# One group of the down projection's weight sums per up step

## The chip, the cores and the metric

One core of one Trainium2 chip runs the whole kernel as one program. The metric is device time in microseconds, the median of several runs. The engines are named as in the profile: PE (TensorE, matrix products; PEld is its loading of weights), DVE (VectorE), ACT (ScalarE), POOL (GpSimd) and SP (SyncE, which here only issues transfers). Each engine works off its own queue in order and waits on semaphores of the others.

## The reference

One inference step of a decoder layer, float32, for 1024 new prompt tokens and 8 decode tokens (1032 columns). Cut to what matters here:

```python
h = rmsnorm(x, norm1_w); proj = h @ w_in               # 1024 -> 6672
...                                                    # two recurrences: Mamba-2 (SSD) and HGRN2, 8 heads
x = x + concat([o_a, y]) @ w_out                       # 2048 -> 1024
h = rmsnorm(x, norm2_w)
gate, val = split(h @ w_up, 2)                         # 1024 -> 2 x 2816
gate = causal_dwconv(gate, ...)                        # width 3
x = x + (silu(gate) * val) @ w_down                    # 2816 -> 1024
y = rmsnorm(x, final_norm_w)
```

The kernel also returns the recurrent and convolution states.

## The kernel before, in words

Activations lie transposed, features on the 128 partitions and the 1032 tokens along the free axis. Each float32 product is made of three passes: a tile is split into a rounded part and a rest (`wh`/`wl` for weights, `uh`/`ul` for activations; ACT copies the rounded part, DVE subtracts it), and wh*uh, wh*ul and wl*uh are added up in PSUM.

The up and the down projection are made by a Strassen-like scheme: 2x2 blocks, seven products p1 to p7 in place of eight, on sums of blocks. The operands of four of the down projection's products (p6, p5, p4, p7) are sums of blocks of `w_down`. They are made ahead of time by `down_sums`: for each of 11 row-block pairs `i` and two halves `h` (22 groups) it loads four 128x256 blocks into the one buffer `wq` (tag "g", one buffer, which later holds the norm's `rst`), adds on POOL four times (L1202), and stores 512 KB to the scratch tensor `wsum_d` (L1204). The down projection reads `wsum_d` back (`dw_load`).

The order of the stages: the combined input projection with the SSD scan beside it; the eight HGRN2 heads, whose small products are put between the input projection's (`drive`); the output projection (jobs a, b, c, d0, d1); the up projection, 22 steps `j` of 128 gate and 128 value columns (`ups`); the down projection; the final norm.

One up step has 14 products of 12 matmuls, in the order p1, p6, p5, p7, p2, p4, p3, each for both halves `i` of the tokens; `n` counts them from 0 to 13. p1, p7 and p3 use the PSUM tag "mm" (three banks, named `ua` in the profile), the others the tag "mx" (four banks, `ub`). DVE or ACT empties each bank (L1463 to L1498). `p7` also makes two subtractions on POOL (L1476, L1477), whose result the p3 product is added to (L1498). During a step the next one is prepared: `up_load(j + 1)` after n = 2 (two loads of 512 KB into `ws`), four sums of these weights on POOL (`up_sums`, L1417), and the splits of them (`up_split`, L1440 on ACT and L1441 on DVE) after n = 5, 9 and 13 and n = 1 of the next step. `up_close` then runs the convolution (L368, L370), SiLU and the gate product, and `act_sets` stores the activations' blocks to `act_d` (L1521).

The order on PE is written out by hand: it is the order of the code. On the other engines and on SP a planner orders the instructions by their place in the code, their due times and its own costs, so an instruction can stand in its queue ahead of one written before it. `tc.issue_after(x.ins)` around an instruction says that it comes after `x` in the queue of `x`'s engine, without a wait of its own. `fetch` issues a load behind the last weight load in SP's queue (`last_w`).

`tick` is called once for each matmul of a step and releases work queued with `after(n, ...)`; `spread(pieces, n)` runs one piece of a generator, and the next n ticks later. A job's step counts as a tick too. Before, `spread(down_sums(), 26)` is begun by the job "conv", ahead of the third head's input projection.

Of the kernel before, what the change touches and what calls it, by code (L numbers as in the profile page):

```python
# [13 lines left out]
ALU = mybir.AluOpType  # L14
# [3 lines left out]
P = 128  # L18
DM = 1024
# [15 lines left out]
DK = FT // 2  # L35
# [16 lines left out]
def hybrid_layer(  # L52
# [9 lines left out]
    V, A, G, PE, SP = nc.vector, nc.scalar, nc.gpsimd, nc.tensor, nc.sync  # L62
# [9 lines left out]
    def nm(s):  # L72
        cnt[0] += 1
        return f"{s}_{cnt[0]}"
# [8 lines left out]
    def tl(tag, name, dt=F32):  # L83
        w, n = TAGS[tag]
        return (work if tag in ("hT", "big", "e", "g") else tmp).tile([P, w], dt, tag=tag, bufs=n, name=nm(name))
# [104 lines left out]
    def fetch(dst, src):  # L190

        with tc.issue_after(last_w[0].ins):
            SP.dma_start(dst, src)  # L193
# [44 lines left out]
    def job(name, load, run):  # L238
        jobs.append((name, load, run))

    def after(n, work):

        item = [n, work]
        later.append(item)
        return item
# [14 lines left out]
    def spread(pieces, n, then=None):  # L260

        def go():
            if next(pieces, 0) is None:
                after(n, go)
            elif then is not None:
                then()
        go()
# [75 lines left out]
    def conv_state(src2d, nrow, ntile, out):  # L343
        def rows(j0):
            rt = half("rt")
            nj = min(4, ntile - j0)
            fetch(rt[:nrow, :nj * P], src2d[:, j0 * P:(j0 + nj) * P])
            return rt, nj

        nxt = rows(0)  # L350
        for j0 in range(0, ntile, 4):
            yield
            (rt, nj), nxt = nxt, rows(j0 + 4) if j0 + 4 < ntile else None
            ps = bank("cst", "nx")
            for j in range(nj):
                PE.transpose(ps[:, j * nrow:(j + 1) * nrow], rt[:nrow, j * P:(j + 1) * P], ident[:nrow, :nrow])
            V.tensor_copy(out[:, j0:j0 + nj, :], ps[:, :nj * nrow].rearrange("p (j r) -> p j r", r=nrow))
# [120 lines left out]
    for i in range(9):  # L478
        n = P if i < 8 else ND
# [285 lines left out]
    def ssm_conv_state():  # L765
        for j0 in range(0, XT, 4):
            yield
            ps = bank("l11", "nx")
            for j in range(4):
                PE.transpose(ps[:11, j * P:(j + 1) * P], last11[:, j0 + j, :], ident)  # L770
            csr = keep.tile([16, 512], F32, tag="csr", bufs=1, name=nm("csr"))
            V.tensor_copy(csr[:11, :512], ps[:11, :])
            cl = slice(j0 * P, (j0 + 4) * P)
            SP.dma_start(cs_prompt[0, 0, :, cl], csr[0:3, :512])
            SP.dma_start(cs_sample[0, :, 2, cl], csr[3:11, :512])
        SP.dma_start(cs_sample[0, :, 0:2, :], state_conv_ssm[0, :, 1:3, :])
# [16 lines left out]
    def once(work):  # L793
        def run():
            work()
            return
            yield
        return run
# [63 lines left out]
    def head_in(h):  # L862
        t = {}

        def f_end():
            f, k = t["f"], tl("big", "k")
            A.activation(f[:, :NT], f[:, :NT], AF.Identity, bias=lbt[:, 0, h:h + 1], scale=lbt[:, 1, h:h + 1])
            V.tensor_scalar(k[:, :NT], f[:, :NT], -1.0, 1.0, op0=ALU.mult, op1=ALU.add)
            t["k"] = k

        for n, off, func in (("f", OFF_F, AF.Sigmoid), ("q", OFF_Q, AF.Silu), ("v", OFF_I, AF.Copy),
                             ("sg", OFF_G, AF.Silu)):
            def evict(c, cs, ps, n=n, func=func):
                t["out"] = A.activation(t[n][:, cs], ps, func)

            def begin(n=n):
                t[n] = tl("e" if h == 0 and n == "f" else "big", n)

            if h == H - 1 and n == "sg":
                in_job_last(f"{n}{h}", off + h * P, evict, begin)  # L880
            else:
                in_job(f"{n}{h}", off + h * P, evict, begin, f_end if n == "f" else None)
        return t
# [305 lines left out]

    wsum_d = dram.tile([2, 4, 2, P, DK, P], F32, name="wsum_d")  # L1190

    def down_sums():
        src = w_down[0].rearrange("(i two p) (gv h c) -> h i p two gv c", two=2, p=P, gv=2, h=2)
        for i in range(DK):
            for h in range(2):
                t = tl("g", "wq")[:, :DM]
                for two in range(2):
                    fetch(t[:, two * 512:(two + 1) * 512].rearrange("p (gv c) -> p gv c", gv=2), src[h, i][:, two])
                yield
                g1, v1, g2, v2 = (t[:, n * 256:(n + 1) * 256] for n in range(4))  # L1200
                for out, x_, y_ in ((v2, v1, v2), (v1, g1, v1), (g1, v2, g1), (g2, g1, g2)):
                    G.tensor_tensor(out, x_, y_, op=ALU.add)  # L1202
                yield
                SP.dma_start(wsum_d[h].rearrange("q m p k c -> p k (q m) c")[:, i],  # L1204
                             t.rearrange("p (q c) -> p q c", c=P))
                yield

    fbufT = keep.tile([P, FT, 16], F32, name="fbufT")

    def conv_states():  # L1210
        yield from ssm_conv_state()
        yield from conv_state(state_conv_ffn[0].rearrange("b r d -> (b r) d"), 16, FT, fbufT)
        yield
# [3 lines left out]
    heads[0] = head_in(0)  # L1217
    ssm_gate(1)
    heads[1] = head_in(1)
    job("conv", None, once(lambda: (spread(conv_states(), 60), spread(down_sums(), 26))))  # L1220
    for h in range(2, H):
        heads[h] = head_in(h)

# [170 lines left out]
    def up_load(j):  # L1394
        ws = []
        for c0 in (0, DFF):
            if j:
                t = wpool.tile([P, KT * P], F32, tag="ws", bufs=2, name=nm("ws"))
            else:
                t = tl("xv", "ws")[:, :KT * P]  # L1400
            last_w[0] = SP.dma_start(t.rearrange("p (k m) -> p k m", m=P),
                                     w_up[0, :, c0 + j * P:c0 + (j + 1) * P].rearrange("(k p) m -> p k m", p=P))
            ws.append(t)
        wraw[j] = ws
        if j > 1:
            up_sums(j)
# [20 lines left out]
    def up_split(j, n):  # L1427

        sums, ops_ = wparts[j]
        order = ORDER if j else FIRST  # L1430
        pool = tmp if n < 2 else wpool
        hi = pool.tile([P, KT * P], F32R, tag="wh", bufs=2, name=nm("wh"))
        lo = pool.tile([P, KT * P], F32R, tag="wl", bufs=2, name=nm("wl"))
        for i, name in enumerate(order[2 * n:2 * n + 2]):
            cs = slice(i * 512, (i + 1) * 512)
            if j == 1:
                with tc.issue_after(setmark[0].ins):
                    A.copy(hi[:, cs], sums[name])
            else:
                A.copy(hi[:, cs], sums[name])  # L1440
            V.tensor_tensor(lo[:, cs], sums[name], hi[:, cs].bitcast(F32), op=ALU.subtract)  # L1441
            ops_[name] = [t[:, cs].rearrange("p (k m) -> p k m", m=P) for t in (hi, lo)]

    class Up:
# [28 lines left out]
        def p7(self, ps):  # L1473
            self.u3 = tl("us", "us")
            V.tensor_tensor(self.u3, self.u2, ps, op=ALU.add)
            G.tensor_tensor(self.val[:, self.at(1)], self.f, self.u3, op=ALU.subtract)  # L1476
            G.tensor_tensor(self.u2, self.f, self.u2, op=ALU.subtract)  # L1477
            if hasattr(self, "late"):
                self.p4(self.late)

# [19 lines left out]
    def up_open(j):  # L1500
        ext, val = tl("xe", "fext"), tl("xv", "val")
        G.memset(ext[:, 0:2], 0.0)
        dreg = ext[:, 2 + T:2 + T + 24].rearrange("p (b r) -> p b r", r=3)
        G.tensor_copy(dreg[:, :, 0:2], fbufT[:, j, :].rearrange("p (b r) -> p b r", r=2))
        return [Up(j, i, ext, val) for i in range(2)]
# [143 lines left out]
    def ups(j, seq):  # L1649

        us_ = up_open(j)
        for n, (name, i) in enumerate(seq):
            yield from us_[i].mul(name)
            if n == 2 and j + 1 < FT:
                up_load(j + 1)
            if n == 5 and j == 0:
                up_sums(1)
            if n in (5, 9, 13) and j + 1 < FT:
                up_split(j + 1, (5, 9, 13).index(n))
            if n == 1 and j:  # L1660
                up_split(j, 3)
            if j == FT - 1:
                last_step(n)
        up_close(j, us_[0])

    with tc.manual_schedule(engines={mybir.EngineType.PE}):
# [26 lines left out]
        for _ in ups(0, [(name, i) for i in range(2) for name in FIRST]):  # L1693
            tick()
# [137 lines left out]
```

## Time and profile before

| | |
|---|---|
| time, median of 3 runs | 1749.66 us (1748.3 to 1752.6) |
| the profiled execution | 1748.51 us, span 1746.6 us |
| granted TensorE clock | 0.998 |
| PE busy | 1704.6 us (98%) |
| DVE busy | 1180.5 us (68%) |
| ACT busy | 838.3 us (48%) |
| POOL busy | 485.6 us (28%) |
| hardware DMA queue | 236.72 MB, 45.1% of 16 engines' span |

The span is the time from the first to the last instruction of the core; the rest of an execution lies around it. A row of a group of instructions names line, engine, operation, what it writes and reads, the shape and how many; then microseconds busy, the mean in nanoseconds, and the engine's idle time before them with what ended it. A row of the timeline begins with start and duration in microseconds. A row of waits names who waited for whom: total, times, longest. SPq rows are transfers being issued. The heads' stage runs from about 428 to 880 us of the span, the up steps from about 1054 to 1482, the down projection behind them.

### The profile page before, as it was taken

Reading aid. Unit: us, or ns where it says so; the run is one execution under the profiler, and the core shown is the slowest. Engines: PE = TensorE matmul, PEld = TensorE weight load, DVE = VectorE, ACT = ScalarE, POOL = GpSimd, SP = SyncE. Lnnn points to the kernel's source line nnn. Section 1 sums busy time; section 2 is a strip of 40 time slices with the busy share of each in tenths; the row PEclk is TensorE's granted clock in tenths of the full one; section 3 lists DMA queues with packets and bytes.
Section 4 is the critical chain, followed back from the end, with each engine's and each line's share of the span. In section 5 each row is a group of like instructions: output and inputs, shape, how many; then the busy total and the mean of one; then the engine's idle time right before and its main releaser. Section 6 shows DMA issues by size and latency. Waiting matters only on the chain.

```text
span 1746.6 us, 39082 instructions
## 1 busy us (share of the span) xinstructions
PE 1704.6 (98%) x15967; PEld 1650.3 (94%) x15967; DVE 1180.5 (68%) x2053; ACT 838.3 (48%) x1507; POOL 485.6 (28%) x500
## 2 busy tenths in 40 slices
PE   7999999999999999999999998999999999999998
PEld 7999998998999999999899998999999999999998
DVE  4657888467755655664755678867777777775664
ACT  6478688443443444444344444334433334444344
POOL 1102242111433422440102124554445554000001
PEclk9999999999999999999999999999999999999999
DMA  5133574563444443444556442323333323786463
GB/s 158 37 82 93 144 211 139 154 178 120 147 140 127 133 147 111 139 131 124 159 169 204 127 136 58 104 92 95 101 113 113 92 92 96 251 270 229 152 190 123
DMA packets 319689, 239.31 MB, mean 137 GB/s; under 512 B 18380, under 2 KB 287734, under 8 KB 319494
## 3 DMA queue, kind: packets, MB, share of 16 engines
q1 hardware_dynamic: 319222, 236.72, 45.1%
q8 instruction: 125, 2.05, 0.5%
q14 instruction: 54, 0.44, 0.1%
q0 software_dynamic: 288, 0.10, 0.0%
HBM read 178.18 MB, written 58.77 MB: 136 GB/s over the span
## 4 chain that ended last, share of the span: by engine, by line
PE 41%; DVE 4%; DMA 2%; ACT 1%; issue 1%; SPq 1%; DVEq 0%; ACTq 0%
PE ub L94 13%; PE dn L94 11%; PE ua L94 9%; PE mm L94 7%; DMA at<-act_d 1%; DMA ws<-in_w_out_dram 1%; DVE x L1320 1%; DVE wl L1094 0%; PE fin L1761 0%; SPq L193 0%; DVE ul L1331 0%; DMA x<-x_d 0%; DVE wl L1441 0%; DMA act_d<-fext 0%; DVE fcv L370 0%
## 5 line engine op out<-in xcount | busy, mean ns | idle before, releaser
L94 PE MATMUL mm<-hh,wh 128*128 128x344 f32 x1248 | 406.5, 326 | 0.0
L94 PE MATMUL mm<-hl,wh 128*128 128x344 f32 x1248 | 403.9, 324 | 0.0
L94 PE MATMUL mm<-hh,wl 128*128 128x344 f32 x1248 | 402.9, 323 | 0.0
L94 PEld LDWEIGHTS mm<-hh,wh 128*128 128x128 f32 x1248 | 234.9, 188 | 2.9 <-issue 0.9
L94 PEld LDWEIGHTS mm<-hh,wl 128*128 128x128 f32 x1248 | 235.1, 188 | 2.1 <-issue 1.0
L94 PEld LDWEIGHTS mm<-hl,wh 128*128 128x128 f32 x1248 | 234.9, 188 | 2.2 <-issue 0.9
L94 PE MATMUL ub<-uh,wh 128*128 128x258 f32 x704 | 199.4, 283 | 2.1 <-DVE fext L1491 1.6
L94 PE MATMUL ub<-ul,wh 128*128 128x258 f32 x704 | 199.6, 283 | 1.5 <-DVE ul L1352 1.5
L94 PE MATMUL ub<-uh,wl 128*128 128x258 f32 x704 | 198.8, 282 | 0.0
L94 PE MATMUL mm<-mx,wh 128*128 128x258 f32 x1024 | 190.9, 286 | 3.2 <-DVE mx L1110 2.3
L94 PEld LDWEIGHTS mm<-mx,wh 128*128 128x128 f32 x1024 | 158.5, 189 | 5.2 <-DVE mx L1110 2.7
L94 PE MATMUL dn<-at,wh 128*128 128x260 f32 (+1 forms) x896 | 163.1, 282 | 0.0
L94 PE MATMUL ua<-uh,wh 128*128 128x258 f32 x528 | 149.2, 283 | 1.1 <-ACT us L1463 0.6
L94 PE MATMUL ua<-ul,wh 128*128 128x258 f32 x528 | 148.9, 282 | 0.0
L94 PE MATMUL ua<-uh,wl 128*128 128x258 f32 x528 | 148.4, 281 | 0.0
L94 PE MATMUL mm<-mx,wl 128*128 128x258 f32 x512 | 145.4, 284 | 1.7 <-DVE wl L1094 1.7
L94 PEld LDWEIGHTS dn<-at,wh 128*128 128x128 f32 x896 | 137.6, 188 | 0.0
L1202 POOL TENSOR_TENSOR wq<-wq 128x256 f32<-128x256 f32 x88 | 83.3, 947 | 189.0 <-DMA wq<-in_w_down_dram 149.6
L94 PEld LDWEIGHTS ub<-uh,wh 128*128 128x128 f32 x704 | 132.9, 189 | 2.5 <-ACT uh L1330 1.8
L94 PEld LDWEIGHTS ub<-ul,wh 128*128 128x128 f32 x704 | 133.1, 189 | 1.9 <-DVE ul L1352 1.9
L94 PEld LDWEIGHTS ub<-uh,wl 128*128 128x128 f32 x704 | 133.1, 189 | 0.0
L94 PE MATMUL dn<-at,wl 128*128 128x260 f32 (+1 forms) x448 | 126.6, 283 | 2.8 <-DVE wl L1607 2.8
(341 smaller groups left out, 3711.9 us busy)
## 6 DMA issues: line engine op xcount, KB each, us to landing
ws<-in_w_in_dram SPq DMA_DIRECT2D x52, 512.0 KB
ws<-in_w_up_dram SPq DMA_DIRECT2D x44, 512.0 KB
at<-act_d SPq DMA_DIRECT2D x77, 258.0 KB
ws<-in_w_out_dram SPq DMA_DIRECT2D x36, 512.0 KB
wq<-in_w_down_dram SPq DMA_DIRECT2D x44, 256.0 KB
wsum_d<-wq SPq DMA_DIRECT2D x22, 512.0 KB
mx<-mix_d SPq DMA_DIRECT2D x32, 258.0 KB
csb<-cs_d SPq DMA_DIRECT2D x32, 256.0 KB
```

The lines of the kernel that those rows point to most:

```text
L94: PE.matmul(out, lhsT, rhs, start=start, stop=stop)
L1202: G.tensor_tensor(out, x_, y_, op=ALU.add)
L1320: V.scalar_tensor_tensor(x_, x_, col("n2", m), rs, op0=ALU.mult, op1=ALU.mult)
```

## The change

The generator takes a list of groups. The first 4 of 22 are still made in the stage of the heads, with one addition per piece and 70 ticks between pieces. The other 18 (`sums_up`) are made by the up steps 1 to 18, one group each: the loads after product n = 3, one addition after each of n = 9, 10, 11 and 12, and the store after n = 1 of the next step. Every addition of these is put behind `subbed`, the last subtraction L1477 made by `p7`, in POOL's queue.

```diff
-    def down_sums():
+    def down_sums(groups):
         src = w_down[0].rearrange("(i two p) (gv h c) -> h i p two gv c", two=2, p=P, gv=2, h=2)
-        for i in range(DK):
-            for h in range(2):
-                t = tl("g", "wq")[:, :DM]
-                for two in range(2):
-                    fetch(t[:, two * 512:(two + 1) * 512].rearrange("p (gv c) -> p gv c", gv=2), src[h, i][:, two])
+        for n in groups:
+            i, h = n // 2, n % 2
+            t = tl("g", "wq")[:, :DM]
+            for two in range(2):
+                fetch(t[:, two * 512:(two + 1) * 512].rearrange("p (gv c) -> p gv c", gv=2), src[h, i][:, two])
+            yield
+            g1, v1, g2, v2 = (t[:, q * 256:(q + 1) * 256] for q in range(4))
+            for out, x_, y_ in ((v2, v1, v2), (v1, g1, v1), (g1, v2, g1), (g2, g1, g2)):
+                if subbed[0] is None:
+                    G.tensor_tensor(out, x_, y_, op=ALU.add)
+                else:
+                    with tc.issue_after(subbed[0].ins):
+                        G.tensor_tensor(out, x_, y_, op=ALU.add)
                 yield
-                g1, v1, g2, v2 = (t[:, n * 256:(n + 1) * 256] for n in range(4))
-                for out, x_, y_ in ((v2, v1, v2), (v1, g1, v1), (g1, v2, g1), (g2, g1, g2)):
-                    G.tensor_tensor(out, x_, y_, op=ALU.add)
-                yield
-                SP.dma_start(wsum_d[h].rearrange("q m p k c -> p k (q m) c")[:, i],
-                             t.rearrange("p (q c) -> p q c", c=P))
-                yield
+            SP.dma_start(wsum_d[h].rearrange("q m p k c -> p k (q m) c")[:, i], t.rearrange("p (q c) -> p q c", c=P))
+            yield
+
+    GROUPS_UP, subbed = 18, [None]
+    sums_up = down_sums(range(2 * DK - GROUPS_UP, 2 * DK))
...
-    job("conv", None, once(lambda: (spread(conv_states(), 60), spread(down_sums(), 26))))
+    job("conv", None, once(lambda: (spread(conv_states(), 60), spread(down_sums(range(2 * DK - GROUPS_UP)), 70))))
...
-            G.tensor_tensor(self.u2, self.f, self.u2, op=ALU.subtract)
+            subbed[0] = G.tensor_tensor(self.u2, self.f, self.u2, op=ALU.subtract)
...
             if n == 1 and j:
                 up_split(j, 3)
+            if n in ((3, 9, 10, 11, 12) if 1 <= j <= GROUPS_UP else ()) + ((1,) if 2 <= j <= GROUPS_UP + 1 else ()):
+                next(sums_up)
```

## The prediction

> **What bounds the kernel now.** I read the busy times first, then the idle time of TensorE by stage, then what ended it, and last one up step instruction by instruction.
>
> ```profile
> span 1746.6 us, 39082 instructions
> ...
> PE 1704.6 (98%) x15967; PEld 1650.3 (94%) x15967; DVE 1180.5 (68%) x2053; ACT 838.3 (48%) x1507; POOL 485.6 (28%) x500
> ```
>
> TensorE (PE) is busy for all but 1746.6 - 1704.6 = 42.0 us. The change alters no product, so it can only take from these 42 us or add to them. The sums run on POOL. A table by stage (PE, PEld, DVE, ACT, POOL busy; clock; DMA share; GB/s) shows where those 42 us do not lie:
>
> ```profile
> 428.00:787.00 359.00, 356.25 (x4587) 339.50 (x4586) 220.30 (x361) 155.90 (x239) 133.51 (x124) 1.00 0.46 135
> 1090.00:1460.00 370.00, 369.51 (x3080) 369.30 (x3080) 273.75 (x479) 142.87 (x259) 183.59 (x190) 1.00 0.32 99
> 1460.00:1540.00 80.00, 77.44 (x645) 76.58 (x643) 60.06 (x108) 36.20 (x59) 14.05 (x15) 1.00 0.67 209
> ```
>
> ```profile
> L1202 POOL TENSOR_TENSOR wq<-wq x88: 724/744/1605, 433.9 to 785.6; 128x256 f32<-128x256 f32 x88
> L193 SPq DMA_DIRECT2D wq<-in_w_down_dram x44: 545/604/1310, 427.8 to 772.6; - x44
> L1204 SPq DMA_DIRECT2D wsum_d<-wq x22: 365/366/393, 437.9 to 786.7; - x22
> ...
>   DMA wq<-in_w_down_dram: 149.6, 15
> ...
> L1202 POOL TENSOR_TENSOR wq<-wq 128x256 f32<-128x256 f32 x88 | 83.3, 947 | 189.0 <-DMA wq<-in_w_down_dram 149.6
> ```
>
> All 88 sums (947 ns each on average, the row of the page) run from 433.9 to 785.6, in the stage of the heads (first row of the table). TensorE idles there for 359.00 - 356.25 = 2.75 us, though POOL waits 149.6 us for the loads of the sums. The stage that receives 18 groups (second row, the up steps) idles 0.49 us in 370. Both are limited by TensorE's own rate. The waits of TensorE in the two, the heads first:
>
> ```profile
> PE a L94 <- DVE q L925: 2.1, 3, 1.2
> PE cst L356 <- DVE od L699: 0.5, 1, 0.5
> ...
> PE ua L94 <- DVE val L1498: 0.5, 1, 0.5
> ```
>
> **What is removed from the heads.** 18 of 22 groups go: 72 additions, 36 loads of 256 KB and 18 stores of 512 KB. None of them is waited for by TensorE directly. What they cost is indirect: the longest of the three waits for the scaled q (1.2 us, ended by L925 at 472.4) looks like this on VectorE (DVE) and POOL:
>
> ```profile
> 470.05 1.22 DVE L924 TENSOR_TENSOR k<-k,tt 128x512 f32<-128x512 f32 x1
> 471.20 1.21 DVE L925 TENSOR_TENSOR q<-q,tt 128x512 f32<-128x512 f32 x1
> ...
> 469.53 3.46 POOL L1202 TENSOR_TENSOR wq<-wq 128x256 f32<-128x256 f32 x3
> ```
>
> Two multiplications of the shape 128x512 take 1.2 us each while the sums run beside them. How fast the same kind of instruction (two inputs in SBUF, 128x512) is when it is undisturbed is the minimum of this group:
>
> ```profile
> L1441 DVE TENSOR_TENSOR wl<-wt,wh x75: 676/1107/1777, 1093.2 to 1456.9; 128x512 fp32r<-128x512 f32 x75
> ```
>
> 0.68 alone, 1.11 at the median, 1.78 at the longest. So in the heads the two lose about 2 x 0.53 = 1.06 us, nearly the whole of that wait of 1.2. Without the sums the wait goes. I take the 2.1 us of waits for q times 18/22, because four groups stay: **-1.7 us**. Bounds: 0 (the waits may be there for the other POOL work of a head, or four groups may fall on just these places) and -2.75 us (all idle time of the stage). SP's queue also loses 54 transfers here; that is worth nothing, since no wait of TensorE in this stage names a transfer.
>
> **What is added to the up steps: POOL.** One group a step, for 18 steps: 4 additions, tied behind the last subtraction of the p7 products (L1477). By the median of L1202 that is 4 x 0.744 = 3.0 us, by the mean 3.8, and at the longest, 1605 ns, 6.4. POOL in a step of the middle, from those subtractions to its next work:
>
> ```profile
> 1235.51 1.20 POOL L1476 TENSOR_TENSOR val<-us,us 128x258 f32<-128x258 f32 x1
> 1236.67 1.19 POOL L1477 TENSOR_TENSOR us<-us,us 128x258 f32<-128x258 f32 x1
> ...
> 1238.71 0.74 POOL L1477 TENSOR_TENSOR us<-us,us 128x258 f32<-128x258 f32 x1
> 1249.07 1.46 POOL L1417 TENSOR_TENSOR wt<-ws 128x512 f32<-128x512 f32 x1 [9.63 <-DMA ws<-in_w_up_dram]
> ```
>
> POOL is empty from 1239.45 to 1249.07, 9.6 us, waiting for the next w_up. The tie puts the group at the start of that hole, and 3.0 to 6.4 us fit. Cost on POOL itself: 0. If the hole were gone, the additions would push the w_up sums (L1417); they are needed for splits of the following step, which is reckoned below under the queue.
>
> **What is added to the up steps: VectorE.** VectorE works in that hole, and two of its instructions there have two inputs in SBUF:
>
> ```profile
> 1240.11 0.69 DVE L1441 TENSOR_TENSOR wl<-ws,wh 128x512 fp32r<-128x512 f32 x1
> 1240.72 0.68 DVE L1441 TENSOR_TENSOR wl<-wt,wh 128x512 fp32r<-128x512 f32 x1
> 1241.33 0.42 DVE L1498 TENSOR_TENSOR val<-us,ua 128x258 f32<-128x258 f32 x1
> ...
> 1243.66 0.28 PE L94 MATMUL ua<-uh,wh 128*128 128x258 f32 x1
> ```
>
> They run undisturbed now, at 0.69 and 0.68, and stand ahead of L1498, which empties the PSUM bank of the first p3 product. The "mm" tag has three banks, used in turn by p1, p7 and p3, so the product that starts at 1243.66 (the second p1 of the next step) takes the bank that L1498 leaves at 1241.33 + 0.42 = 1241.75. The slack is 1.91 us. With POOL beside them the two splits go from 0.68 to the median 1.11, 0.86 us together: L1498 ends 0.86 later and 1.05 us of slack is left. TensorE loses 0. Upper bound: both at the longest, 2 x (1.777 - 0.68) = 2.2 us, which is 0.3 more than the slack, so 0.3 us for each of 17 steps, 5 us. I take the median, since half of this group, which meets POOL's w_up sums and subtractions all through the stage, take that or less. L370 and the later L1441, which follow, are delayed too, but they feed the conv of a finished step, and the page puts no wait of TensorE behind them in this stage.
>
> The Trainium skill ("SBUF — State Buffer", section "Who interferes with whom") says that a VectorE instruction with two SBUF inputs and a POOL instruction that reads SBUF lock each other out for a whole instruction. By that rule each of the two splits waits at most for one addition, 2 x 0.74 = 1.5 us, under the slack of 1.91, and the steady steps would cost nothing even at worst; the 1.11 and 1.78 above agree with the kind of delay, the longest being beside longer POOL instructions than these.
>
> The first step of the receiving stage has no such slack. At its end the same instructions stand so:
>
> ```profile
> 1100.70 0.80 DVE L1441 TENSOR_TENSOR wl<-ws,wh 128x512 fp32r<-128x512 f32 x1
> 1101.42 0.68 DVE L1441 TENSOR_TENSOR wl<-wt,wh 128x512 fp32r<-128x512 f32 x1
> 1102.02 0.41 DVE L1498 TENSOR_TENSOR val<-us,ua 128x258 f32<-128x258 f32 x1
> ```
>
> Here TensorE already waits 0.5 us for L1498 (the wait quoted above). The group of this step is tied right ahead, so every delay of the two splits passes to TensorE: (1.11 - 0.80) + (1.11 - 0.68) = 0.74, **+0.7 us**; bounds 0 and 2.1 (both at 1.78).
>
> **What is added to the up steps: SP and the transfers.** Two loads and a store a step. SP's queue in this step, and a store in the heads with the next load that had to wait for it (there is one wq buffer):
>
> ```profile
> 1240.87 4.81 SPq L1401 DMA_DIRECT2D ws<-in_w_up_dram  x2
> ...
> 1085.52 0.38 SPq L1401 DMA_DIRECT2D ws<-in_w_up_dram  x1
> ...
> 1247.21 0.81 SPq L1521 DMA_DIRECT2D act_d<-val  x2
> ...
> 473.83 0.37 SPq L1204 DMA_DIRECT2D wsum_d<-wq  x1
> ...
> 477.15 1.21 SPq L193 DMA_DIRECT2D wq<-in_w_down_dram  x2
> ```
>
> A store takes 477.15 - 473.83 = 3.3 us until its buffer is free. It waits for the four additions (1239.45 + 4 x 0.95 = 1243.3), and in a queue it holds up what stands behind: the second w_up load, which its buffer lets go at 1245.3 anyway (the end of the first row, less the 0.38 of one issue), then the act_d stores. If the planner puts it first, the first w_up load leaves at 1243.7 instead of 1240.87, still ahead of the second. The second may land up to 3.3 us late for sharing the engines with the store, and so may the sums on POOL and the subtractions L1476 and L1477. The first L1477 ends at 1237.86 and L1498 needs it at 1241.33: 3.4 us of room, and the 1.91 of the bank behind it. So a delay of 3.3 costs 0. The bytes: 18 x 1.0 MB (two loads and a store) in 370 us bring 99 GB/s to 150 and the share of 0.32 to about 0.5, which is the 0.46 at which the heads run now with no wait of TensorE for a transfer. The act_d stores go 1 to 3 us later; their tiles are taken again a step (20 us) on. Cost 0; bounds 0 and what the second rival gives.
>
> **The rest.** The head stage's four groups are spaced 70 ticks with 6 pieces each, 4 x 6 x 70 = 1680 ticks against 22 x 3 x 26 = 1716, so they end where the sums end now. The last store belongs to up step 19; the first use of wsum_d is in step 21, 20 us or more later: 0. The third row of the table, the last up step and what follows, sees none of it: 0.
>
> **The sum.** -1.7 + 0.7 = -1.0 us on the profiled execution of 1748.51 us, which is 1.15 us under the median of 1749.66; so 1747.5 beside that execution and 1748.7 us as a median.
>
> **The rivals.**
> *VectorE becomes late in every step* (slower). Place: the two splits ahead of L1498. It decides from a delay of 1.91 us per step; each tenth beyond costs 17 x 0.1 = 1.7 us. At the longest rows (2.2) it is +5, 1754; with one more 0.68 split moved in front by the planner, 0.6 beyond, +10, 1759. For it: VectorE is 74% busy here (273.75 of 370), and the slack of 1.91 is the smallest I found. Against it: the median delay is 0.86.
>
> *The queue of SP becomes late* (slower). A store that waits for stretched additions holds the w_up loads. It decides when the second load lands more than 3.4 + 1.91 = 5.3 us late; the additions would have to end after 1247.3, 2.0 us each, and the longest is 1.605. Past that point each us costs 18: at 1 us beyond, 1766. Against it: two rows must be beyond their extremes.
>
> *The heads gain more.* All of 2.75 us, and the waits of TensorE from 787 to 900 shrink with queues that run ahead:
>
> ```profile
> PE mm L94 <- DVE mx L1110: 2.3, 2, 1.3
> PE a L94 <- issue: 1.7, 1, 1.7
> PE a L94 <- DVE q L925: 0.9, 2, 0.7
> ```
>
> These are 4.9 us; with 3 to 4.9 of them gone beside 2.75, 1742 to 1744. For it: SP's in-order queue holds loads behind those of wq. Against it: the last sum starts at 785.6.
>
> *The tie does not hold the place.* "Behind the subtraction" is a lower bound; the planner may put the additions among the sums of w_up at 1249. Then 4 x 0.95 = 3.8 us push L1476 and L1477 by more than 3.4, the bank takes the remaining 0.4: 0 in the up steps, 1749.7 - 1.7 = 1748.
>
> **How the numbers follow.** The forecast 0.60; VectorE late 0.18; SP late 0.10; more gain 0.08; the tie 0.04. Within 0.3% (1744.4 to 1754.9, about what a measurement of this kernel can tell from no change) lie the forecast but for 0.02 at each edge, half of VectorE late, and the tie: 0.56 + 0.09 + 0.04 = 0.69. Slower: half of VectorE late, SP late and the upper edge, 0.09 + 0.10 + 0.02 = 0.21. Faster: more gain and the lower edge, 0.10. The range, 1744 to 1758, leaves out SP late (0.10), the end of VectorE late (some 0.03) and of more gain (0.04). The forecast's own range is 1746 (all 2.75 us, nothing lost) to 1752 (no gain, 2.1 lost).
>
> **What would show it.** Right: the heads' wait of a for L925 falls below 1 us; POOL's busy time from 1090 to 1460 rises by about 68 us (72 x 0.947) and TensorE there stays at 99.8%; L1441 ahead of L1498 at about 1.1; one wait for val L1498 of about 1.2 us at the first step. Wrong: repeated waits of ua for L1498, or of ub and ua for splits, spaced 20 us apart; the w_up loads leaving more than 5 us later in their step.

## The result, and the profile after

The changed kernel takes 1802.22 us (median of 6, 1800.69 to 1803.98), the kernel before beside it 1752.15: a ratio of 1.0289, 95% interval 1.0273 to 1.0306. It is 2.9% slower; forecast were 1748.7 and a range from 1744 to 1758. One of the six executions of the kernel before took 7989.54 us and is left out of the ratio.

In the changed kernel the lines behind the change have other numbers: the sums of `wq` are L1203 (heads) and L1206 (up steps), their store L1208, the w_up loads L1407, their sums L1423, the splits L1446 (ACT) and L1447 (DVE), the emptying of p5 L1477 and of p3 L1504, the subtractions of p7 L1482 and L1483, the stores of `act_d` L1527.

The page and the table by stage (PE, PEld, DVE, ACT, POOL busy; clock; DMA share; GB/s) of the changed kernel:

```profile
span 1799.0 us, 39031 instructions
...
PE 1721.6 (96%) x15967; PEld 1661.1 (92%) x15967; DVE 1184.3 (66%) x2053; ACT 834.7 (46%) x1507; POOL 518.5 (29%) x500
...
428.00:787.00 359.00, 358.48 (x4716) 341.38 (x4717) 203.65 (x365) 157.36 (x239) 63.14 (x52) 1.00 0.29 84
1090.00:1460.00 370.00, 335.40 (x2700) 329.89 (x2699) 254.23 (x417) 119.25 (x220) 241.14 (x222) 0.99 0.47 132
1135.50:1138.80 3.30, 3.07 (x14) 3.07 (x15) 3.30 (x6) 1.62 (x4) 3.30 (x5) 0.50 0.00 0
```

The heads are better: TensorE idles 0.5 us there, where it idled 2.75. The up steps are where it goes wrong: TensorE idles 34.6 us in a stretch in which it idled 0.49. From the beginning of up step 1 to that of step 21 the first products of the traces lie 404.7 us apart before and 460.7 after, 56 us more; steps 4 to 19 take 23.38 us on average in place of 20.15. Who TensorE waits for there:

```profile
PE ub L94 <- ACT us L1477: 24.9, 17, 2.6
PE ua L94 <- DVE val L1504: 17.1, 14, 1.3
```

That is 42.0 us in 31 waits. Four stretches of 3.4 us at half clock (the row of 0.50 is one) lie between 1100 and 1545 us and cost some 4 x 1.7 = 6.8. The other 7 us would be about 0.23 for each wait; in part one sees them in the first product after it, 0.39 in place of 0.28 us.

One cycle of POOL's timeline, from the additions of one step to those of the next:

```profile
1281.41 5.73 POOL L1206 TENSOR_TENSOR wq<-wq 128x256 f32<-128x256 f32 x4
1294.54 1.28 POOL L1423 TENSOR_TENSOR wt<-ws 128x512 f32<-128x512 f32 x1 [7.39 <-DMA ws<-in_w_up_dram]
...
1298.36 1.75 POOL L1423 TENSOR_TENSOR wt<-wt,ws 128x512 f32<-128x512 f32 x1
1300.07 1.19 POOL L1482 TENSOR_TENSOR val<-us,us 128x258 f32<-128x258 f32 x1
...
1303.26 1.21 POOL L1483 TENSOR_TENSOR us<-us,us 128x258 f32<-128x258 f32 x1
1304.44 5.72 POOL L1206 TENSOR_TENSOR wq<-wq 128x256 f32<-128x256 f32 x4
```

and SP's queue in the same time:

```profile
1287.17 0.37 SPq L1208 DMA_DIRECT2D wsum_d<-wq  x1
1287.64 1.94 SPq L1407 DMA_DIRECT2D ws<-in_w_up_dram  x2
1290.88 0.55 SPq L193 DMA_DIRECT2D wq<-in_w_down_dram  x1
1291.54 4.02 SPq L1527 DMA_DIRECT2D act_d<-val  x8
```

The additions end at 1287.14; 0.03 us later SP issues the store that waited for them, and directly behind it the two w_up loads, which stood in the queue behind the store. The loads let POOL's sums begin at 1294.54; the subtractions of p7 come behind the sums, and the next additions are tied behind the subtractions: 5.7 + 7.4 + 5.5 + 4.4 = 23.0 us, one step. The chain ends where it began.

How TensorE comes to wait is in rows of ACT, PE and VectorE of the same step:

```profile
1297.20 0.62 ACT L1446 CAST wh<-wt 128x512 fp32r<-128x512 f32 x1 [3.57 <-POOL wt L1423]
1297.73 0.37 ACT L1477 COPY us<-ub 128x258 f32<-128x258 f32 x1
...
1298.15 0.39 PE L94 MATMUL ub<-uh,wh 128*128 128x258 f32 x1 [1.05 <-ACT us L1477]
...
1303.80 1.22 DVE L1447 TENSOR_TENSOR wl<-wt,wh 128x512 fp32r<-128x512 f32 x1
1304.94 0.41 DVE L1504 TENSOR_TENSOR val<-us,ua 128x258 f32<-128x258 f32 x1
...
1305.41 0.39 PE L94 MATMUL ua<-uh,wh 128*128 128x258 f32 x1 [1.26 <-DVE val L1504]
```

The second p5 bank (L1477) stands in ACT's queue behind the cast of a weight sum that POOL has not made yet, and the second p4 product needs that bank. VectorE too waits for that cast, until 1297.85, and from there works without a pause up to the first p3 bank (L1504), which stands behind the splits L1447 in its queue. The subtraction that L1504 needs (the first L1483) had ended by 1302.41 and was not what held it.

### The profile page after: what moved, and what is told of

Same layout as the page of the kernel before. It is cut to its first block, busy times and chain, and to the rows that moved or that the text cites. A ratio compares the mean times of both kernels' runs of the same rounds, so it can differ in the third digit from the quotient of the medians.

```text
span 1799.0 us, 39031 instructions
## 1 busy us (share of the span) xinstructions
PE 1721.6 (96%) x15967; PEld 1661.1 (92%) x15967; DVE 1184.3 (66%) x2053; ACT 834.7 (46%) x1507; POOL 518.5 (29%) x500
## 4 chain that ended last, share of the span: by engine, by line
PE 20%; POOL 11%; DMA 7%; issue 7%; DVE 5%; ACT 1%; SPq 1%; DVEq 0%; POOLq 0%; ACTq 0%
PE dn L94 10%; PE mm L94 7%; POOL wq L1206 5%; DMA act_d<-val 2%; POOL us L1483 2%; DMA wq<-in_w_down_dram 2%; POOL wt L1423 2%; POOL val L1482 1%; DMA wsum_d<-wq 1%; PE ub L94 1%; SPq L1527 1%; PE ua L94 1%; DVE wl L1447 1%; DMA ws<-in_w_out_dram 1%; DVE fcv L370 1%
## 5 line engine op out<-in xcount | busy, mean ns | idle before, releaser
L94 PE MATMUL ub<-uh,wh 128*128 128x258 f32 x704 | 203.4, 289 | 27.1 <-ACT us L1477 24.9
L94 PE MATMUL ua<-uh,wh 128*128 128x258 f32 x528 | 153.2, 290 | 17.5 <-DVE val L1504 17.1
L1447 DVE TENSOR_TENSOR wl<-wt,wh 128x512 fp32r<-128x512 f32 x88 | 92.3, 1069 | 69.5 <-ACT wh L1446 69.5
```

What stands on the lines that cost most here:

```text
L94: PE.matmul(out, lhsT, rhs, start=start, stop=stop)
```

## The experiments

Three theories were tried against each other. *Loop*: additions, store, w_up loads, sums and subtractions form a closed chain of 23 us, longer than the 20.15 us of TensorE's products. *Port*: POOL's additions slow VectorE, and VectorE holds TensorE. *Traffic*: 18.9 MB more in the up steps make the w_up loads late. The lengths of the cycle's parts are means over POOL's timeline, 13 cycles from the group of step 4 to that of step 17; "step" is the mean distance of the first products of up steps 4 to 20. POOL does its work once a step, so the parts add up to about a step in every kernel, waits included; that sum alone shows no closed chain. What tells is whether a part that is made longer or shorter shows whole in the step, and whether the step goes back to 20.15 when one link is taken out. Results with an interval are medians of 6 or 10 executions; each of the others is a single execution.

| kernel | additions | to the first sum | sums | to and in subtractions | together | step | time |
|---|---|---|---|---|---|---|---|
| changed | 5.73 | 7.70 | 5.57 | 4.31 | 23.31 | 23.38 | 1802.22 |
| small additions | 2.52 | 7.89 | 5.60 | 4.31 | 20.32 | 20.32 | 1745.31 |
| twice the additions | 9.54 | 7.86 | 5.54 | 4.30 | 27.24 | 27.26 | 1871.42 |
| small store | 5.73 | 5.47 | 5.60 | 4.32 | 21.11 | 21.09 | 1762.76 |
| store of another tile | 5.51 | 4.84 | 5.71 | 4.02 | 20.08 | 20.18 | 1745.61 |
| store behind the loads | 5.21 | 5.21 | 5.74 | 3.98 | 20.13 | 20.15 | 1744.53 |

**The store behind the w_up loads.** The call for the store moves from n = 1 to n = 2, behind `up_load`, and the store is tied behind the last load:

```diff
-            SP.dma_start(wsum_d[h]...[:, i], t...)
+            with tc.issue_after(last_w[0].ins):        # up steps only
+                SP.dma_start(wsum_d[h]...[:, i], t...)
...
-... + ((1,) if 2 <= j <= GROUPS_UP + 1 else ()):
+... + ((2,) if 2 <= j <= GROUPS_UP + 1 else ()):
```

> The store of a group is built after the next w_up loads and put behind them in SP's queue; additions, tie and bytes stay. Loop theory: in the changed kernel a step's work closes a loop, additions 5.7 us, then store and w_up loads behind it until the sums can start 7.4, sums 5.6, subtractions 4.4, together 23.0 us against the 20.15 of TensorE's products; with the loads no longer behind the store the loop is open, the steps go back to 20.15 us and the time to 1744 to 1750. Port theory (the additions slow VectorE's instructions, and these hold TensorE): additions and tie are as before, so it stays at 1790 to 1805. Traffic theory (18.9 MB more in these steps delay the w_up loads): same bytes, 1785 to 1805.

Measured: 1744.53 us beside 1748.09, ratio 0.9979 (0.9964 to 0.9994). SP's queue and POOL in one step, and the table of stages:

```profile
1240.94 5.52 SPq L1411 DMA_DIRECT2D ws<-in_w_up_dram  x2
1246.66 0.42 SPq L1212 DMA_DIRECT2D wsum_d<-wq  x1
...
1240.89 5.75 POOL L1206 TENSOR_TENSOR wq<-wq 128x256 f32<-128x256 f32 x4
1250.30 1.30 POOL L1427 TENSOR_TENSOR wt<-ws 128x512 f32<-128x512 f32 x1 [3.66 <-DMA ws<-in_w_up_dram]
...
1090.00:1460.00 370.00, 370.00 (x3086) 370.00 (x3085) 289.48 (x479) 142.24 (x259) 273.58 (x260) 1.00 0.49 148
```

The first w_up load leaves while the additions run, at 1240.94. The four additions shown take as long as in the changed kernel (on the mean 5.2 us in place of 5.7), and TensorE has no idle time at all in 370 us, though POOL is busy 273.58 and 148 GB/s are moved. Port and traffic fall as the cause; neither the additions nor the bytes cost anything where the loop is open.

**Small additions.** `G.tensor_tensor(out[:, :16], x_[:, :16], y_[:, :16], ...)` in the up steps.

> The 72 additions of the up steps work on 16 of 256 columns, so the sums are incomplete; queues and transfers stay as in the changed kernel. Loop theory: the loop loses 5.7 us less four short instructions of some 0.1, about 17.7 us, under 20.15, so the steps take 20.15 and the time is 1743 to 1750. Port theory: also about 1745. Traffic theory: unchanged, 1795 to 1805.

Measured: 1745.31 us. All other parts of the cycle stay; with 3.2 us less in the additions the step comes to 20.32 on the mean, and 13 of the 16 steps take 20.15 or 20.16: the chain is then about as long as TensorE's products. Traffic falls here as well (same bytes). The additions are longer than I expected, 0.6 in place of 0.1 us (last section), which is why the chain is not the 17.7 us expected.

**Twice the additions.** Behind each `G.tensor_tensor(out, x_, y_)` a `G.tensor_tensor(out, out, y_)`.

> Each of the 72 additions is followed by a second one of the same shape, so the sums are other sums; the rest stays. Loop theory: everything added to the loop shows in each step, four times 1.2 to 1.43 us or 4.9 to 5.8 per step, 17 to 18 steps: 1885 to 1905. Port theory: what follows the additions in VectorE's queue is late, but the longer additions run beside the conv and not beside the splits ahead of L1504: 1805 to 1830. Traffic theory: unchanged, 1800.

Measured: 1871.42 us, 14 under the range. The additions take 9.54 in place of 5.73, 3.81 more and not 4.9 to 5.8, because half of the additions, the second of each pair, take 0.81 us at the median. These 3.81 us appear whole in the step: 27.26 against 23.38. The port theory (1805 to 1830) is far off.

**Small store.** 64 of 512 KB of each group: `SP.dma_start(wsum_d[h]...[:, i, 0:1], t...[:, 0:1])`, and `src = wsum_d[m // 2, 0, 0]` for all sums.

> The store of a group in the up steps writes 64 of 512 KB, and the down projection reads one block of the sums in place of all, so the output is another; the store's place in SP's queue, ahead of the w_up loads, and its wait for the additions stay. Loop theory: only the part of the 7.4 us that comes from sharing the engines goes, 1 to 3 us of 23.0, so steps of 20.2 to 22 us and 1745 to 1780. Port theory: 1800. Traffic theory: 8.3 of 18.9 MB go, so some 45% of the loss, 1775 to 1780.

Measured: 1762.76 us. From the end of the additions to the first sum it takes 5.47 us in place of 7.70. So 2.2 us of the loop are the store's bytes in front of the loads, and its place in the queue still costs 21.09 - 20.15 = 0.94 us a step.

**Store of another tile.** Same place in the order of SP's queue, same bytes, but the source is a tile of activations, so nothing waits for the additions:

```diff
+                other = usets[1]["p2"][0]...[:, :DM].bitcast(F32)
+                with tc.issue_after(last_f[0].ins):    # the last fetch
+                    SP.dma_start(wsum_d[h]...[:, i], other...)
```

> The store of a group stands at the same place in SP's queue, ahead of the w_up loads, and moves the same 512 KB, but from a tile of the activations, so it doesn't wait for the additions and the stored blocks are not the sums; additions, tie and loads stay. Loop theory: the loop is open, steps of 20.15 us, 1742 to 1750. Traffic theory (the store's bytes just ahead of the w_up loads are what costs): 1775 to 1800. Port theory: 1790 to 1800.

Measured: 1745.61 us, steps of 20.18. It is the wait for the additions, in front of the w_up loads, that closes the loop; without it the same 512 KB, still ahead of the loads, cost nothing. They leave early, though: in one step the store is issued at 1246.47 and the next loads at 1257.19, so this run does not test bytes moved beside the loads; the small store does that. Nor does the store hold the buffer `wq` here, and with it the next group's loads. In the two kernels that take the store from in front of the w_up loads (above, and from POOL's queue below) it still holds `wq`, and there too the steps take 20.15 and 20.17 us, so the buffer does not close the loop.

**Without the tie.** The additions are not put behind `subbed`.

> The additions of the up steps are no longer tied behind the p7 subtractions; the store stays ahead of the w_up loads. The planner now puts, in every other step, three of the four additions before the last two subtractions or all four of them, and behind all in the others. Loop theory: the loop still runs through additions, store, loads and sums, and is shorter by one pair of subtractions (2.0 us) in every other step, so 22.3 us on average and 1765 to 1790. If the tie closes the loop: 20.15 us and 1743 to 1750.

Measured: 1785.49 us, steps of 22.26. In every other step two of the four subtractions now come behind the last addition and so outside the chain. The tie lengthens the loop and is not its cause.

**The heads alone.** The 18 groups are left out of the whole kernel, and `dw_load` reads blocks of `w_down` for all sums.

> The 18 groups are not made at all, and the down projection reads blocks of w_down in place of all sums; this is the removal from the heads alone. If what the traces show between the first and the last head (4.7 us less) comes from the removal: 1741 to 1745 beside 1748. If it was a difference from execution to execution: 1746 to 1749. The forecast's term was -1.7 us.

Measured: 1745.30 us beside 1747.66, ratio 0.9988 (0.9978 to 0.9998): a gain of 2.4 us. The time lies between the two ranges expected; the next trace tells more.

**The kernel before, once more.**

> The kernel before, once more, for a second trace of it: from the first to the last head 380.9 us again, against 376.2 in all kernels without the 18 groups there, if the groups are the reason; the wait of 2.2 us for q at 398, before the first group, is there or not.

Measured: 1744.99 us in this execution. From the second to the last head (from one's first product `vd` to the other's) its trace has 381.3 us (380.9 in the first trace), against 376.2 to 376.5 in all the kernels without the 18 groups there. The waits of TensorE from 428 to 787 us in this second trace, then the only one left in the kernel with the groups left out:

```profile
PE a L94 <- DVE q L925: 1.7, 3, 1.1
PE a L94 <- issue: 1.3, 1, 1.3
PE cst L356 <- DVE od L699: 0.5, 1, 0.5
...
PE cst L356 <- DVE od L699: 0.5, 1, 0.5
```

The waits for q and the one that the profile puts down to "issue" go with the groups; the wait at 398 is there in both (0.6 and 1.3 us in these two), and is not theirs.

**The store from POOL's queue.** `G.dma_start` for the store of the up steps in place of `SP.dma_start`.

> The 18 stores of the up steps are issued from POOL's own queue, right behind the additions, in place of SP's. SP's queue then holds nothing that waits for the additions ahead of the w_up loads. Loop theory: the loop is open, steps of 20.15 us, 1742 to 1750, as long as POOL issues a store in less than the 4 to 5 us that it is idle in a step. If what costs is POOL's work in a step as such (port, or its sums coming late): 1780 to 1805.

Measured: 1745.94 us beside 1750.26, ratio 0.9977 (0.9964 to 0.9989), steps of 20.17. POOL spends 0.9 us on each:

```profile
L1208 POOL DMA_DIRECT2D wsum_d<-wq x18: 899/904/993, 1101.4 to 1447.0; - x18
...
1090.00:1460.00 370.00, 368.75 (x3072) 368.33 (x3071) 295.16 (x484) 141.72 (x256) 300.48 (x277) 1.00 0.49 148
```

POOL is busier here than in the changed kernel (300.48 against 241.14 us) and costs nothing. A second way to take the store from in front of the loads has the same effect.

**The store behind the loads, again.**

> The kernel with the store behind the w_up loads, once more, for a narrower interval beside the kernel before: 1743 to 1747, 0.1 to 0.3% under it, since the heads without the 18 groups were worth 2.4 us alone and the up steps cost nothing.

Measured: 1743.85 us beside 1750.26, ratio 0.9959 (0.9944 to 0.9974). The gain of 0.4% is above the 0.1 to 0.3% expected. This version is a little faster than the kernel before, and 58 us faster than the changed one.

## Why the prediction was wrong, point by point

**SP and the transfers: this step failed.** The prediction had the store wait for the additions, it had the w_up loads behind the store, and it had a load 3.3 us late; it then said "So a delay of 3.3 costs 0.", because there were 3.4 us of room before L1498 and 1.91 behind. Room absorbs a delay that comes once. This one comes back: late loads make late sums, late subtractions, and, by the tie, late additions, and the store of the next step waits for those. What counts in such a chain is its whole length against the 20.15 us of a step, not the room at one place. The prediction's own rows gave it: additions 3.8, the store 3.3, a load 3.8 (1245.3 to 1249.07), from the first sum to the subtractions 6.6 (1249.07 less a step, to 1235.51), the subtractions 3.9: 21.4, more than 20.15. The measured 23.3 has 5.7 for the additions and less for the sums.

**The second rival** was the right place and far too dear a condition: it asked that the additions end after 1247.3, two us each. They took 1.43 each, and that was enough, since the delay did not have to arise in one step: it grows from step to step until the loop sets the pace. Its price, "each us costs 18", held: 3.81 us more gave 69.2 us more, 18.2 for each.

**A wait left out.** Of 42.0 us, 24.9 are for the p5 bank that ACT empties behind a cast. Named behind POOL's sums were only the subtractions and L1498; what stands behind a waiting cast in ACT's queue was not looked at. The cycle of 23.3 sets the time whichever of the two banks is late, so this changes how TensorE waits and not how long a step is; with the small store 10.2 of 11.4 us were for the p3 bank, and the step still followed the loop.

**The heads, -1.7 us.** Right in kind, by the waits for q that vanish, and somewhat small: -2.4 us alone. The 1.3 to 1.7 us put down to "issue" were not in this term (the third rival had them). In the traces the heads from the second to the last are 4.4 to 5.1 us shorter, more than the medians move. For one pair of traces the rest can be found: the kernel with the groups left out has three stretches of 3.4 us at a clock of 0.50 (at 291, 830 and 1527), some 5.1 us lost, and the second trace of the kernel before has none before its last 10 us; their spans are 1743.5 and 1743.1. Whether that holds for the medians is not shown. The four groups left in the heads begin their last addition at 694.6 and not at 785.6, where the prediction had them end with the sums of the kernel before.

**POOL, 0.** Right, where the loop is open: the additions fit the hole. By the mean of 0.947 they were 3.8 us; they took 5.2 to 5.7, inside the bound of 6.4.

**VectorE, 0 in the steady steps.** Right: no wait for the p3 bank in 370 us with the store behind the loads, nor in the kernel with the other tile, and with the store from POOL's queue only the one at the first step. The Trainium skill's rule ("SBUF — State Buffer", section "Who interferes with whom") pointed the same way, and the traces agree (last section). The meeting had its effect where it was not looked for: it lengthens the additions from 3.0 to 5.7 us, and without that the loop would by this sum be 20.6. The +0.7 at the first step came where TensorE reached it at full clock: with the store from POOL's queue the wait there is 1.2 us, 0.7 more than the 0.5 before. In the changed kernel and in the first trace with the store behind the loads no wait stands there; both have a stretch at a clock of 0.50 shortly ahead of it (at 1067 and 1076), so TensorE comes later.

**The bytes, 0.** Right in the open loop, at 148 GB/s and a share of 0.49. In the closed one the store's are 2.2 of the 23.3 us.

**The rival of more gain in the heads** reached 1742 to 1744; the two opened versions come to 1743.85 to 1745.94, 3.6 to 6.4 us under the kernel before beside them, so one of the three measurements lies inside it. From 787 to 900 the waits it listed come to 4.9 and 3.5 us in the two traces of the kernel before and to 1.9 to 3.6 in those without the 18 groups there; it needed 3 to 4.9 of them gone.

**The tie** held its place: in all 18 steps the four additions follow the last subtraction.

## What to carry to other kernels

When a queue in order gets an instruction that waits for another engine, follow what stands behind it until the chain ends or comes back to the waiting instruction. If it comes back in the next step, add up the whole chain and compare it with the step; slack at single places says nothing then, and each us above costs as many us as there are steps. A store that waits for fresh results belongs behind the loads of the next step or in the queue of the engine that makes the results; moving one transfer was worth 56 to 58 us here (1802.22 against 1743.85 to 1745.94).

## What the runs showed of the hardware

Half clock after short waits, but not after each. In the changed kernel a single wait of TensorE of 2.2 to 2.6 us was followed by 3.4 us at a granted clock of 0.50 (the row 1135.50:1138.80 above, after a wait of 2.3 us at 1133), four times; steps with two waits of 1.0 to 1.4 us, 7 us apart, had no such stretch. The length of a wait does not decide it alone. Without the tie there are six waits of 2.12 to 2.13 us, and one of them was followed by such a stretch, while a wait of 1.81 us in the same trace was; with twice the additions a wait of 3.45 us (ending at 1359.8) was followed by full clock. The Trainium skill ("TensorE: Matmul & The Clock Gate", section "Why this matters for your kernels") sets the limit at idle gaps of about 3 us between matmul bursts; here shorter ones were sometimes enough, and one longer gap did not do it.

Additions behind VectorE's instructions. At the median an addition of 16 columns beside VectorE costs nearly what one of 256 costs alone:

```profile
L1206 POOL TENSOR_TENSOR wq<-wq x72: 219/605/1180, 1093.7 to 1441.7; 128x16 f32<-128x16 f32 x72
...
L1206 POOL TENSOR_TENSOR wq<-wq x72: 1058/1406/1631, 1094.6 to 1495.9; 128x256 f32<-128x256 f32 x72
```

The first row is of the kernel with the small additions, the second of the changed one. It shows 0.22 us at the least and 0.61 at the median. The difference is a wait for an instruction of VectorE to end. Of these 72 additions, 35 start while no VectorE instruction with two inputs in SBUF is running, and all of them take 0.22 us. The other 37 start while one is running (L1447 or L370), and each ends 0.08 us after it does. L1504, which reads one of its inputs from PSUM, does not hold them up.

The 256 columns show the same. All 72 additions of the changed kernel's up steps start while such an instruction runs and end 0.58 to 0.61 us after it. With the store behind the loads 8 of 72 start free of one and take 0.73 to 0.75 us; the other 64 end 0.59 to 0.61 us after the one that was running. So an addition that starts then makes little or no headway until the VectorE instruction has ended.
